# Attention gate bias on GpSimd: one operation on negated rows becomes two operations on rows as they are

## The chip, the core and the metric

The kernel runs on one core of a Trainium2 chip. The metric is device time in microseconds (us) of one execution. The core has four compute engines that run side by side and wait for each other through semaphores: PE (TensorE, matrix products; the profile lists its weight loads apart as PEld), DVE (VectorE), ACT (ScalarE) and POOL (GpSimd). SP issues the DMA transfers.

## What is computed

Two layers on 1024 tokens of width 1024. Layer 0 is a convolution module with a feed-forward net behind it, layer 1 an attention layer with another. The change lies in the attention, which has 16 heads of width 64 and a learned forget gate:

```python
log_f = log_sigmoid(f_logit + b_f)
c = cumsum(log_f, axis=1)                  # c[head, token]
s = q @ k.T                                # q is scaled by HEAD_DIM ** -0.5
bias = c[t] - c[s]                         # query t, key s
s = where(k_pos <= q_pos, s + bias, NEG_BIG)
o = softmax(s) @ v
```

## The kernel before, in words

`attention` works through 64 units: 8 head pairs p, in each four blocks u of 256 queries (from the longest row of keys to the shortest, in the last pair the other way round), and both heads e of the pair. A unit has two query tiles b of 128 queries; the tile i = 2u + b needs W = (i + 1) x 128 key columns, so W runs over 128, 256, ... 1024, each of them 16 times.

`gates` makes the cumulative gates once. `ctok` keeps them with tokens on partitions (128 x 8 x 16), and a transpose makes one row for each head, which goes to a buffer `cd` in DRAM (line 617 evacuates the transpose from PSUM, line 618 stores). For each head pair `gate_rows` loads each of the two rows from there, broadcast to 128 partitions, as `cb` (128 x 1024).

`scores` then does the softmax of a unit. For each of its two query tiles the work goes round the engines:

- POOL, line 709: z = row of gates + the query's gate (a column of 128 values), W columns. z is the buffer `pr`.
- POOL, line 710: the causal mask is added to the last 128 columns of z.
- PE, lines 718 and 719: two products of up to 512 columns into a PSUM tile `s` (three buffers).
- DVE, line 723: z = -(s + z) with the running minimum in `sm`; this frees `s`. Line 728 takes the smaller of two minima.
- ACT, line 729: exp, with the sum; DVE, line 730: its reciprocal.
- POOL, line 731: z times the reciprocal, times 1.0. Source and destination are the same buffer.

`values` follows a unit later: PE transposes the tiles (line 779, tile `t`), ACT and DVE split them into a high and a low part (`pt`, lines 111 and 112), POOL clears the part above the diagonal (line 781), and PE multiplies with V (line 749, tile `po`). In between, the units of pairs 0 to 6 are filled with the projections of the next pair (`psv`, `psq`, `psk`, line 137), which need no result of the softmax. Their weights pass through POOL too (line 125, times a gain). The last pair has no next one to project; it has the first part of the output product (`ps_wo`) beside and behind it.

Each engine runs its instructions in a fixed order. That order is not written in the code: a scheduler in the compiler lays it out from the units' priorities and from its own idea of how long each instruction takes, so an edit to one instruction can move others.

Of the kernel before, what the change touches and what calls it, by code (L numbers as in the profile page):

```python
# [14 lines left out]
ALU = mybir.AluOpType  # L15
# [7 lines left out]
HB = 512  # L23
# [36 lines left out]
class K:  # L60
# [521 lines left out]
    def gates(self, cd):  # L582

        nc = self.nc
        g = self.at.tile([P, T - P], F32, name="gate0", tag="pr0")
        gr = self.at.tile([P, T], F32, name="gate1", tag="pr1")
        u, e, lt, x = (g[:, i * P : (i + 1) * P] for i in range(4))
        z = self.zf.rearrange("p b n -> p (b n)")

        nc.vector.tensor_scalar(u, z, -1.0, None, ALU.mult)  # L590
        nc.vector.tensor_tensor(u, u, z, ALU.min)
        nc.scalar.activation(e, u, AF.Exp)
        nc.vector.tensor_scalar(u, e, 1.0, None, ALU.add)
        nc.scalar.activation(lt, u, AF.Ln)
        nc.vector.tensor_scalar(z, z, 0.0, None, ALU.min)
        nc.vector.tensor_tensor(z, z, lt, ALU.subtract)
        nc.vector.scalar_tensor_tensor(e, u, -1.0, e, ALU.add, ALU.subtract)
        nc.vector.reciprocal(lt, u)
        nc.vector.tensor_tensor(e, e, lt, ALU.mult)
        nc.vector.tensor_tensor(z, z, e, ALU.add)  # L600

        N = NHEAD
        nc.vector.tensor_copy(x[:, N : 2 * N], z[:, 0:N])
        for b in range(2, KT):
            c = b * N
            nc.vector.tensor_tensor(x[:, c : c + N], x[:, c - N : c], z[:, c - N : c], ALU.add)
        st = self.stp.tile([P, HB], F32, name="st_c", tag=self.stt)
        nc.tensor.matmul(st[:, 0:P], self.tri, z, start=True, stop=False)
        nc.tensor.matmul(st[:, N:P], self.ones, x[:, N:P], start=False, stop=True)
        ctok = self.cp.tile([P, KT, N], F32, name="ctok")  # L610
        nc.vector.tensor_copy(ctok.rearrange("p b n -> p (b n)"), st[:, 0:P])
        rows = gr[0:N, :]
        for h in range(NH):
            st = self.stp.tile([P, HB], F32, name=f"st_r{h}", tag=self.stt)
            for b in range(4):
                nc.tensor.transpose(st[0:N, b * P : (b + 1) * P], ctok[:, 4 * h + b, :], self.ident)
            nc.scalar.mul(rows[:, h * HB : (h + 1) * HB], st[0:N, :], -1.0)
        nc.sync.dma_start(cd, rows)
        return ctok

# [76 lines left out]
    def scores(self, cur, p, e, u):  # L697

        nc = self.nc
        n = 2 * p + e  # L700
        qk, ql = cur[p]
        cb = cur[p, "cb"][e]
        pr = [self.at.tile([P, T - (1 - b) * P], F32, name=f"pr{n}{u}{b}", tag=f"pr{b}") for b in range(2)]
        for b in range(2):
            i = 2 * u + b
            W = (i + 1) * P
            q = slice(i * P, W)
            z = pr[b][:, 0:W]
            nc.gpsimd.tensor_scalar(z, cb[:, 0:W], self.ctok[:, i, n : n + 1], None, ALU.add)  # L709
            nc.gpsimd.tensor_tensor(z[:, W - P : W], z[:, W - P : W], self.mask, ALU.add)  # L710
            sm = self.tp.tile([P, 8], F32, name=f"sm{n}{i}", tag="sm", bufs=6)
            m = 0
            for lo in range(0, W, HB):
                hi = min(lo + HB, W)
                cols = max(hi - lo, 256)
                ps = self.sp.tile([P, HB], F32, name=f"s{n}{i}{lo}", tag="s")
                kk = slice(lo, lo + cols)
                nc.tensor.matmul(ps[:, 0:cols], qk[:, e, q], qk[:, 2 + e, kk], start=True, stop=False)
                nc.tensor.matmul(
                    ps[:, 0:cols], ql[:, e, q], qk[:, 2 + e, kk], start=False, stop=True  # L720
                )
                zz = z[:, lo:hi]
                nc.vector.tensor_tensor_reduce(  # L723
                    zz, ps[:, 0 : hi - lo], zz, -1.0, 3.0e38, ALU.add, ALU.min, sm[:, m : m + 1]
                )
                m += 1
            if m == 2:
                nc.vector.tensor_tensor(sm[:, 0:1], sm[:, 0:1], sm[:, 1:2], ALU.min)  # L728
            nc.scalar.activation(z, z, AF.Exp, bias=sm[:, 0:1], scale=-1.0, accum_out=sm[:, 2:3])  # L729
            nc.vector.reciprocal(sm[:, 3:4], sm[:, 2:3])  # L730
            nc.gpsimd.tensor_scalar(z, z, sm[:, 3:4], 1.0, ALU.mult, ALU.mult)  # L731
        return pr
# [144 lines left out]
```

## Time and profile before

| what | value |
|---|---|
| three timed runs | 2718.55, 2723.5 and 2723.99 us, median 2723.5 us |
| the profiled execution, its own time | 2726.07 us |
| its span in the trace | 2724.3 us |
| mean granted clock of TensorE | 0.968 of full speed |
| busy share of the span: PE, DVE, ACT, POOL | 94%, 57%, 37%, 29% |
| units of attention, first to last line-709 instruction | 1243.8 to 1804.0 us |

The last row is the place of the change: 128 instructions of line 709 lie in some 560 us of the span, and POOL is all but idle after that. A busy share over the whole span says little there, so the rows below are cut to that stretch.

### The profile page before, as it was taken

To read this page: it belongs to the slowest core of one execution; us is meant where nothing else is said; L and a number is where in the kernel's file an instruction comes from. 1 tells how busy PE (TensorE), PEld (TensorE's weight loads), DVE (VectorE), ACT (ScalarE), POOL (GpSimd) and SP (SyncE) were. 2 spreads that over 40 slices of the span, in tenths; PEclk is the share of its full clock that TensorE was granted. 3 is DMA by queue.
4 is the path that set the end of the run, shared out by engine and by line. 5 is a ranking of instruction groups with operands and counts; after the bars stand their busy time and mean duration, and the time that the engine had idled before them with its cause. 6 is when DMAs were issued, how large, how long until landed. Compare 5 with 4: busy or idle time off the path is not lost.

```text
span 2724.3 us, 31354 instructions
## 1 busy us (share of the span) xinstructions
PE 2565.2 (94%) x12056; PEld 2133.0 (78%) x12056; DVE 1548.7 (57%) x2535; ACT 1005.9 (37%) x1608; POOL 780.1 (29%) x657
## 2 busy tenths in 40 slices
PE   7996999999999999989998898789999999999996
PEld 6875778888888888878777777568888888888885
DVE  7998999426644445555756666666422323223456
ACT  5245423223423334244545555544311302113232
POOL 3473534443000000025777777650000000000000
PEclk9997999999999999989999999789999999999998
DMA  3124222222222222222111111212111111111132
GB/s 127 54 78 155 70 90 89 105 96 88 99 101 93 101 94 100 74 98 71 47 40 47 40 53 55 103 54 79 48 54 47 47 49 52 47 47 51 54 112 108
DMA packets 63973, 205.25 MB, mean 75 GB/s; under 512 B 7360, under 2 KB 12096, under 8 KB 63312
## 3 DMA queue, kind: packets, MB, share of 16 engines
q1 hardware_dynamic: 62672, 199.06, 20.7%
q10 hardware_dynamic: 1152, 4.19, 0.4%
q8 instruction: 95, 1.56, 0.2%
q14 instruction: 54, 0.44, 0.0%
HBM read 182.71 MB, written 20.51 MB: 75 GB/s over the span
## 4 chain that ended last, share of the span: by engine, by line
PE 78%; DVE 10%; POOL 4%; issue 3%; ACT 2%; DMA 2%; POOLq 0%; DVEq 0%; SPq 0%; ACTq 0%
PE ps_fb L137 25%; PE ps_fa L137 24%; PE ps_gt L137 6%; PE ps_wo L137 3%; DVE ya L331 3%; PE pg L137 3%; PE pa L137 3%; PE psv L137 3%; PE psq L137 2%; PE psk L137 2%; POOL pr L709 2%; PE ps_pw L137 2%; PE t L779 1%; PE po L749 1%; DVE pr L723 1%
## 5 line engine op out<-in xcount | busy, mean ns | idle before, releaser
L204 POOL TENSOR_TENSOR r_g<-ms_g,mhalf 128x4 f32<-128x4 f32 x4 | 5.3, 1326 | 1041.6 <-DVE ms_g L202 1041.6
L331 DVE SCALAR_TENSOR_TENSOR ya<-u,wdw,ya 128x512 f32<-128x512 f32 x420 | 284.2, 746 | 0.0
L111 ACT CAST wh_fb<-raw_fb 128x1024 fp32r<-128x1024 f32 x96 | 101.0, 1054 | 412.2 <-PE ps_fb L137 295.3
L383 DVE SCALAR_TENSOR_TENSOR fa<-ps_fa,bs_f 128x512 f32<-128x512 f32 x128 | 88.0, 691 | 279.0 <-PE ps_fa L137 268.7
L111 ACT CAST wh_fa<-raw_fa 128x1024 fp32r<-128x1024 f32 x96 | 101.1, 1053 | 358.1 <-PE ps_fa L137 175.5
L709 POOL TENSOR_SCALAR pr<-cb,ctok 128x896 f32<-128x896 f32 (+7 forms) x128 | 223.5, 1755 | 33.8 <-PE t L779 29.2
L137 PE MATMUL ps_fa<-f10xl,wh_fa 128*128 128x512 f32 x512 | 199.4, 389 | 0.0
L137 PE MATMUL ps_fa<-f10xh,wl_fa 128*128 128x512 f32 x512 | 199.3, 389 | 0.0
L137 PE MATMUL ps_fa<-f10xh,wh_fa 128*128 128x512 f32 x512 | 199.0, 389 | 0.0
L389 DVE TENSOR_TENSOR hTb<-ps_fb,hTb 128x512 f32<-128x512 f32 x64 | 44.3, 692 | 233.3 <-PE ps_fb L137 233.3
L749 PE MATMUL po<-pt,V 128*128 128x256 f32 x640 | 127.7, 317 | 19.5 <-ACT pt L111 8.5
L385 ACT ACTIVATE fa<-fa 128x512 f32<-128x512 f32 x128 | 80.2, 629 | 153.3 <-DVE fa L383 153.3
L112 DVE TENSOR_TENSOR pt<-t,pt 128x512 fp32r<-128x512 f32 (+1 forms) x160 | 98.8, 633 | 62.6 <-ACT pt L111 62.0
L729 ACT ACTIVATE pr<-pr,sm 128x896 f32<-128x896 f32 (+7 forms) x128 | 99.3, 776 | 86.8 <-DVE sm L728 52.8
L389 DVE TENSOR_TENSOR hT<-ps_fb,hT 128x512 f32<-128x512 f32 x64 | 44.1, 690 | 147.7 <-PE ps_fb L137 147.7
L731 POOL TENSOR_SCALAR pr<-pr,sm 128x896 f32<-128x896 f32 (+7 forms) x128 | 101.6, 799 | 90.7 <-DVE sm L730 77.3
L779 PE MATMUL t<-ident,pr 128*128 128x128 f32 x576 | 103.6, 298 | 24.6 <-POOL pr L731 13.5
L749 PEld LDWEIGHTS po<-pt,V 128*128 128x128 f32 x640 | 98.6, 205 | 34.8 <-ACT pt L111 14.5
L723 DVE CUSTOM_DVE_ANT_0 pr<-s,pr 128x512 f32<-128x512 f32 (+3 forms) x192 | 104.0, 552 | 36.4 <-POOL pr L710 14.8
L111 ACT CAST pt<-t 128x512 fp32r<-128x512 f32 (+1 forms) x160 | 84.1, 543 | 87.1 <-PE t L779 83.9
L137 PEld LDWEIGHTS ps_fa<-f10xl,wh_fa 128*128 128x128 f32 x512 | 96.1, 188 | 20.0
L137 PEld LDWEIGHTS ps_fa<-f10xh,wh_fa 128*128 128x128 f32 x512 | 96.1, 188 | 20.0
(356 smaller groups left out, 7430.8 us busy)
## 6 DMA issues: line engine op xcount, KB each, us to landing
raw_fa<-in_wf SPq DMA_DIRECT2D x96, 512.0 KB, 3.2
raw_fb<-in_wf SPq DMA_DIRECT2D x96, 512.0 KB, 3.2
raw_gt<-in_wgate SPq DMA_DIRECT2D x24, 512.0 KB, 3.2
proj<-pj SPq DMA_DIRECT2D x32, 256.0 KB, 2.2
raw_pw<-in_wpw SPq DMA_DIRECT2D x16, 512.0 KB, 3.3
lpj<-proj SPq DMA_DIRECT2D x32, 256.0 KB, 3.2
cb<-cd SPq DMA_DIRECT2D x16, 512.0 KB, 3.9
raw_wo<-in_wo SPq DMA_DIRECT2D x16, 320.0 KB, 2.8
```

What stands on the lines that cost most here:

```text
L111: copy(h, src)
L112: sub.tensor_tensor(l, src, h.bitcast(F32), ALU.subtract)
L137: self.nc.tensor.matmul(ps, p[:, k, :], q[:, k, :], start=(start and k == k0 and n == 0), stop=(stop and k == kt - 1 and n == 2),)
L331: nc.vector.scalar_tensor_tensor(d, s(j), w(j), o, ALU.mult, ALU.add)
L383: nc.vector.scalar_tensor_tensor(t, ps, 0.0, s[h][1], ALU.max, ALU.mult)
L389: nc.vector.tensor_tensor(hT[h][:, j, :], ps, hT[h][:, j, :], ALU.add)
L709: nc.gpsimd.tensor_scalar(z, cb[:, 0:W], self.ctok[:, i, n : n + 1], None, ALU.add)
L723: nc.vector.tensor_tensor_reduce(zz, ps[:, 0 : hi - lo], zz, -1.0, 3.0e38, ALU.add, ALU.min, sm[:, m : m + 1])
L729: nc.scalar.activation(z, z, AF.Exp, bias=sm[:, 0:1], scale=-1.0, accum_out=sm[:, 2:3])
L731: nc.gpsimd.tensor_scalar(z, z, sm[:, 3:4], 1.0, ALU.mult, ALU.mult)
L749: nc.tensor.matmul(po, V[:, j, n % 4, :], pt[:, q, c : c + 256], start=(j == 0 and q == 0), stop=(jp == u and jj == 1 and q == 1),)
L779: nc.tensor.transpose(ps[:, c : c + P], pr[b][:, j * P : (j + 1) * P], self.ident)
```

## The change

Line 617 stores the gate rows as they are, no longer times minus one. Line 709 makes up for it: it multiplies the row by minus one and adds the query's gate, in one instruction. Both forms give c[t] - c[s].

```diff
@@ gates
-            nc.scalar.mul(rows[:, h * HB : (h + 1) * HB], st[0:N, :], -1.0)
+            nc.scalar.copy(rows[:, h * HB : (h + 1) * HB], st[0:N, :])
@@ scores
-            nc.gpsimd.tensor_scalar(z, cb[:, 0:W], self.ctok[:, i, n : n + 1], None, ALU.add)
+            nc.gpsimd.tensor_scalar(z, cb[:, 0:W], -1.0, self.ctok[:, i, n : n + 1], ALU.mult, ALU.add)
             nc.gpsimd.tensor_tensor(z[:, W - P : W], z[:, W - P : W], self.mask, ALU.add)
```

The number of instructions of the two lines stays: 2 of line 617 on ACT, 128 of line 709 on POOL. No buffer, transfer or wait is added. The scheduler's order does change on all engines from the first unit on. Two places show how.

On POOL, at the start of attention (head pair 0; `pr030` is head 0, u = 3, b = 0, `raw_q1` and `raw_k1` are weights of the next pair; the number behind the last underscore only tells buffers apart). A minus is the order before, a plus the order of the change:

```order
 L709 TENSOR_SCALAR pr030_8715<-cb0_8711,ctok_8553 128x896
 L709 TENSOR_SCALAR pr031_8716<-cb0_8711,ctok_8553 128x1024
+L710 TENSOR_TENSOR pr030_8715<-pr030_8715,mask_8154 128x128
 L709 TENSOR_SCALAR pr130_8816<-cb1_8713,ctok_8553 128x896
 L709 TENSOR_SCALAR pr131_8817<-cb1_8713,ctok_8553 128x1024
+L710 TENSOR_TENSOR pr031_8716<-pr031_8716,mask_8154 128x128
 L125 TENSOR_TENSOR raw_q1_9273<-raw_q1_9273,vec_66 128x1024
-L710 TENSOR_TENSOR pr030_8715<-pr030_8715,mask_8154 128x128
-L710 TENSOR_TENSOR pr031_8716<-pr031_8716,mask_8154 128x128
```

The two masks of the first unit move ahead of the weights of the next pair, and so do the scores that wait for them.

On POOL, at the end of attention (head pair 7, u = 3, its longest rows):

```order
 L709 TENSOR_SCALAR pr1430_14222<-cb14_13909,ctok_8553 128x896
 L709 TENSOR_SCALAR pr1431_14223<-cb14_13909,ctok_8553 128x1024
+L731 TENSOR_SCALAR pr1521_14148<-pr1521_14148,sm155_14166 128x768
+L710 TENSOR_TENSOR pr1430_14222<-pr1430_14222,mask_8154 128x128
+L710 TENSOR_TENSOR pr1431_14223<-pr1431_14223,mask_8154 128x128
 L781 MEMSET pt1522_14283 128x2x128
 L709 TENSOR_SCALAR pr1530_14295<-cb15_13911,ctok_8553 128x896
 L709 TENSOR_SCALAR pr1531_14296<-cb15_13911,ctok_8553 128x1024
-L710 TENSOR_TENSOR pr1430_14222<-pr1430_14222,mask_8154 128x128
-L710 TENSOR_TENSOR pr1431_14223<-pr1431_14223,mask_8154 128x128
```

Here the masks of head 14 no longer stand behind the two line-709 instructions of head 15.

## Rows read from the trace of the kernel before

**Rows 1.** The page's busy line; then busy us by engine, clock, DMA in three stretches:

```profile
span 2724.3 us, 31354 instructions
...
PE 2565.2 (94%) x12056; PEld 2133.0 (78%) x12056; DVE 1548.7 (57%) x2535; ACT 1005.9 (37%) x1608; POOL 780.1 (29%) x657
...
1225.00:1825.00 600.00, 525.10 (x2945) 440.16 (x2944) 382.91 (x967) 314.38 (x641) 438.70 (x467) 0.93 0.16 56
1275.00:1675.00 400.00, 360.35 (x2099) 306.29 (x2098) 257.88 (x645) 211.87 (x428) 302.19 (x317) 0.97 0.12 42
1675.00:1825.00 150.00, 115.63 (x531) 89.40 (x530) 97.33 (x266) 79.53 (x177) 112.37 (x135) 0.81 0.24 87
```

**Rows 2.** Chain of work that ended last, share by line, 1225-1825 us and 1675-1825 us:

```profile
by line: PE psq L137 10.5%; PE psk L137 10.3%; POOL pr L709 8.5%; issue 8.1%; PE psv L137 7.9%; PE t L779 5.8%; PE po L749 5.6%; DVE pr L723 3.2%; PE s L718 3.1%; POOL pr L731 3.1%; PE s L719 2.7%; PE ps_wo L137 2.6%; DVE pt L112 2.3%; ACT 
by line: POOL pr L709 10.9%; PE ps_wo L137 10.3%; issue 7.9%; DMA raw_o<-od 6.8%; PE psk L137 5.4%; POOL pr L731 5.2%; PE po L749 5.2%; DMA cb<-cd 5.0%; PE t L779 4.4%; DVE pr L723 4.3%; DMA od<-o 4.0%; DVE xol L112 3.9%; ACT pr L729 3.7%; 
```

**Rows 3.** Lines 709 and 731, whole and by shape: count, busy us, mean ns, idle before:

```profile
L709 POOL TENSOR_SCALAR pr<-cb,ctok 128x896 f32<-128x896 f32 (+7 forms) x128 | 223.5, 1755 | 33.8 <-PE t L779 29.2
...
L731 POOL TENSOR_SCALAR pr<-pr,sm 128x896 f32<-128x896 f32 (+7 forms) x128 | 101.6, 799 | 90.7 <-DVE sm L730 77.3
...
L709 POOL TENSOR_SCALAR pr<-cb,ctok 128x1024 f32<-128x1024 f32 x16 | 45.6, 2850 | 0.0
L709 POOL TENSOR_SCALAR pr<-cb,ctok 128x512 f32<-128x512 f32 x16 | 25.1, 1566 | 0.6 <-PE t L779 0.6
L709 POOL TENSOR_SCALAR pr<-cb,ctok 128x128 f32<-128x128 f32 x16 | 9.7, 608 | 8.3 <-PE t L779 6.6 <-DMA cb<-cd 1.7
L731 POOL TENSOR_SCALAR pr<-pr,sm 128x1024 f32<-128x1024 f32 x16 | 18.9, 1181 | 25.8 <-DVE sm L730 19.9 <-DVE sm L728 5.6
L731 POOL TENSOR_SCALAR pr<-pr,sm 128x512 f32<-128x512 f32 x16 | 11.4, 712 | 7.1 <-DVE sm L730 7.1
L731 POOL TENSOR_SCALAR pr<-pr,sm 128x128 f32<-128x128 f32 x16 | 6.1, 379 | 2.8 <-DVE sm L730 2.7
```

**Rows 4.** Other two-input POOL instructions by shape, adding (323, 710) and multiplying (304, 300):

```profile
L323 POOL TENSOR_TENSOR y<-y,cm 128x512 f32<-128x512 f32 x30 | 42.8, 1426 | 5.1 <-ACT cm L321 3.5
L304 POOL TENSOR_TENSOR ta<-ta,bs_n 128x512 f32<-128x512 f32 x16 | 24.2, 1514 | 20.6 <-ACT ta L303 20.6
L300 POOL TENSOR_TENSOR sg<-sg,bs_n 128x512 f32<-128x512 f32 x16 | 21.2, 1322 | 12.1 <-ACT sg L299 8.8 <-ACT bs_n L210 3.3
L710 POOL TENSOR_TENSOR pr<-pr,mask 128x128 f32<-128x128 f32 x128 | 64.1, 512 | 0.0
```

**Rows 5.** Timeline of POOL late in attention: start, duration, line:

```profile
1781.35 2.21 POOL L709 TENSOR_SCALAR pr<-cb,ctok 128x768 f32<-128x768 f32 x1
1783.54 0.70 POOL L731 TENSOR_SCALAR pr<-pr,sm 128x512 f32<-128x512 f32 x1
1784.20 0.88 POOL L710 TENSOR_TENSOR pr<-pr,mask 128x128 f32<-128x128 f32 x2
1785.06 1.89 POOL L709 TENSOR_SCALAR pr<-cb,ctok 128x640 f32<-128x640 f32 x1
1786.89 0.31 POOL L781 MEMSET pt<- 128x256 f32 x1
1787.18 2.21 POOL L709 TENSOR_SCALAR pr<-cb,ctok 128x768 f32<-128x768 f32 x1
```

**Rows 6.** Waits in attention: engine and line, released by, total us, times, longest:

```profile
PE s L718 <- DVE sm L723: 21.3, 25, 3.5
PE t L779 <- POOL pr L731: 13.5, 16, 2.5
PE t L779 <- DVE pt L112: 8.7, 21, 1.3
PE po L749 <- ACT pt L111: 8.5, 13, 1.6
...
DVE pr L723 <- POOL pr L710: 14.8, 22, 2.1
DVE pr L723 <- POOL pr L709: 9.0, 11, 1.5
```

**Rows 7.** ACT: the evacuation at line 617, and a plain copy from PSUM:

```profile
L617 ACT ACTIVATE gate<-st_r x2: 589/589/589, 1234.4 to 1237.1; 16x512 f32<-16x512 f32 x2
...
L299 ACT COPY sg<-pg 128x512 f32<-128x512 f32 x16 | 9.3, 580 | 22.6 <-PE pg L137 20.5 <-DVE acc_n L196 1.8 <-DVE u L305 0.3
```

## Prediction

> **What bounds the kernel now.** I read first the busy line of the page, then the busy time cut to the stretch in which line 709 runs [rows 1]. Over the whole span POOL is busy 29% and looks harmless. Between 1225 and 1825 us it is busy 438.7 of 600 us, second only to PE with 525.1. PE therefore stands idle 600 - 525.1 = 74.9 us there. That is the most that any change to the softmax's side work can return as idle time. The idle time is uneven: 400 - 360.4 = 39.6 us between 1275 and 1675 us, where the projections of the next pair fill PE, and 150 - 115.6 = 34.4 us between 1675 and 1825 us, where that filling gives out. There the granted clock also falls to 0.81, from 0.97.
>
> Next I read the chain of waits, to see whether POOL's busy time sits on the path that sets the end [rows 2]. It does: line 709 has 8.5% of the chain in the 600 us, or 51.0 us, and 10.9% of the 150 us at the end, or 16.4 us, where it is the largest entry of all. Last I read who waits for POOL [rows 6]. PE waits for line 731 before its transposes (13.5 us), and for line 723 to free a score tile (21.3 us). Line 723 itself is held by lines 710 and 709 (14.8 and 9.0 us). So line 709 hurts mostly through what is queued behind it on POOL, not by direct waits.
>
> **What the change removes, step by step.** *The bias instruction.* Line 709 takes 223.5 us of POOL in 128 instructions; line 731 has the same eight shapes, 16 of each, and takes 101.6 us [rows 3]. Both are a POOL tensor_scalar on f32 in SBUF with a column operand. From 128 to 1024 columns line 709 goes from 608 to 2850 ns, 2.50 ns a column; line 731 goes from 379 to 1181 ns, 0.90 ns a column. So on this engine the form with two operations is already seen to be the cheaper one, by almost three times a column. The question is which difference between the two lines makes it so. They differ in the number of operations (one against two), in the kind (add against multiply), in the buffer (from `cb` to `pr` against in place), and in the place of the column operand. The new form agrees with line 731 in the number of operations and in its first operation; it differs in the other three.
>
> The kind alone is a poor explanation: on two-input instructions of 512 columns an add takes 1426 ns and two multiplies 1322 and 1514 ns [rows 4], so adding isn't dearer as such. Contention for the memory is a poor one too: late in attention, line 709 with 768 columns takes 2.21 us both times, and the next instruction starts right behind it, so the duration is real, and a line-731 instruction of 512 columns in between takes 0.70 us under the same neighbours [rows 5]. In place or not, and where the column stands, no row separates.
>
> So the bounds for the new form are: below, line 731's 101.6 us in all; above, a generic loop that pays for each operation, up to twice line 709's price a column. Twice means 2.50 ns x 576 columns on average x 128 = 184 us more. I take the lower bound, since line 731 is the nearest row in every respect that changes: 223.5 - 101.6 = 121.9 us less POOL, 54.5% of line 709.
>
> The Trainium skill has a rule that speaks against this. GPSIMD Engine Reference, section Performance versus the Vector engine, says that a loop with up to two operations an element runs at the memory port's rate, 1.03 cycles an element, and gets slower only from three on. By it a second operation can't make anything faster, and line 709 should already cost what line 731 does; a change of the operation count would then return nothing. The trace agrees for line 731 and disagrees for line 709, which takes nearly three times as long; the measurement decides that the one-operation form isn't at that rate here, but not why.
>
> *The path.* Of the 51.0 us of line 709 on the chain, 54.5% go: 27.8 us. Two things are left out on either side. What is late next takes some of it back: the transposes also wait for line 112 (8.7 us) and the products with V for line 111 (8.5 us) [rows 6], and a shorter POOL step uncovers them. Against that, PE waits less and may keep its clock in the last 150 us, where 0.81 is granted. I set these two equal. For the range, half of the 27.8 us (14) is lost to the next waits at worst, and at best two thirds of PE's idle time (50 us) come back.
>
> *The gate rows.* Line 617 becomes a copy, twice in the program. It took 589 ns as a multiply; a plain copy from PSUM with the same 512 columns takes 580 ns [rows 7]. I count nothing; even 1 us each would be hidden, as PE still has projections to run there.
>
> *The order.* The scheduler moves instructions on all engines. On POOL the masks move ahead of the second head's line 709 and ahead of the weights of the next pair. Each shift puts at most two or three POOL instructions before another, some 2 to 5 us by rows 3 and 4, and it shortens the way to line 723 as often as it delays weights, so I count nothing and keep +-5 us for the range.
>
> **The sum.** 2726.1 - 27.8 = 2698.3 us for the profiled execution. That one lies 2.6 us above the median of the three timed runs, so the forecast for a median is 2723.5 - 27.8 = 2696 us, 1.0% faster. About 0.2%, 5 us, is what a measurement of this kernel can tell from no change.
>
> **The rivals.**
>
> *The second operation costs extra (slower).* Line 709 may be slow because its add with a column runs in a generic loop; the new form then stays in that loop and pays for another operation. At line 731's 0.90 ns a column this adds 0.90 x 576 x 128 = 66 us of POOL, 23% of which reach the chain as now (51.0 / 223.5): +15 us, 2739 us. At double price POOL would need 438.7 + 184 = 623 us in the 600 us: it becomes the bound, and by its share of the chain +42 us, 2766 us. It decides as soon as the new form costs more than 2.50 ns a column by some 0.3 (5 us at the chain's share). For it: lines 709 and 731 differ in three more things than the count. Against it: no row shows a POOL tensor_scalar with two operations slower than one.
>
> *The duration doesn't change.* Slowness comes from reading one buffer and writing another, or from the column added to; this is what the rule above would leave as the cause. Then only the order moves: 2723 us, 5 either way.
>
> *Faster on POOL, nothing at the end.* The POOL step shortens, but PE is then held by lines 111 and 112 and by the single `po` tile. For it: PE is already 88% busy in the stretch. Against it: in the last 150 us line 709 tops the chain and PE idles 34.4 us, so that 16.4 x 0.545 = 9 us should return there alone. It gives 2718 to 2724 us.
>
> **How the numbers follow.** The forecast with its gain above 5 us: 0.70, with its own range 2674 to 2710 us (50 and 14 us of gain). Extra cost: 0.12. Unchanged duration: 0.10, of which 0.06 within 0.2%, and 0.02 to each side from the order. Faster POOL without effect: 0.08, of which 0.01 ends slower. So faster 0.70 + 0.02 = 0.72, same 0.06 + 0.07 = 0.13, slower 0.12 + 0.02 + 0.01 = 0.15. The range is 2674 to 2730 us: below it some 0.05, above it the extra cost, 0.12 and a little.
>
> **What would show it.** In the profile of the changed kernel: line 709 at some 800 ns mean and 100 us in all, with 1.2 us for 1024 columns; POOL some 317 us busy in the attention stretch; line 709's share of the chain there halved; PE idle some 50 us in place of 74.9, most of the gain spread over 1275 to 1675 us and a third in the last 150; line 731's duration unchanged. The forecast is wrong if line 709 stays above 1.7 us on average (first or second rival), or if it falls and PE's waits for lines 111, 112 and 723 grow by as much (the third).

## The result, and the profile after

The changed kernel takes 2640.4 us (2639.8 to 2641.8, four runs), where the kernel before takes 2722.3 us (four runs): a ratio of 0.970, with a 95% interval of 0.9685 to 0.9719. It is 82 us faster. The forecast had the direction and the instruction right, but only a third of the gain, and the time lies below its range.

The page and the rows by shape of the kernel after answer to [rows 1] and [rows 3]:

```profile
span 2640.1 us, 31431 instructions
...
PE 2524.8 (96%) x12056; PEld 2113.2 (80%) x12056; DVE 1545.3 (59%) x2535; ACT 1002.3 (38%) x1608; POOL 660.7 (25%) x657
...
L731 POOL TENSOR_SCALAR pr<-pr,sm 128x896 f32<-128x896 f32 (+7 forms) x128 | 98.1, 768 | 101.0 <-DVE sm L730 94.9
...
L709 POOL TENSOR_SCALAR pr<-cb,ctok 128x896 f32<-128x896 f32 (+7 forms) x128 | 105.6, 830 | 36.6 <-PE t L779 31.0
...
L709 POOL TENSOR_SCALAR pr<-cb,ctok 128x1024 f32<-128x1024 f32 x16 | 20.3, 1271 | 0.0
L709 POOL TENSOR_SCALAR pr<-cb,ctok 128x512 f32<-128x512 f32 x16 | 13.8, 863 | 0.0
L709 POOL TENSOR_SCALAR pr<-cb,ctok 128x128 f32<-128x128 f32 x16 | 8.7, 544 | 4.1 <-PE t L779 2.2 <-DMA cb<-cd 1.9
```

Line 709 falls from 223.5 to 105.6 us, 117.9 us less, where 121.9 was forecast; line 731 stays. So the step on the instruction holds. The surprise is elsewhere. Next, busy us by engine, granted clock and DMA of the kernel after in its attention stretch, in the part that projections fill and in the part where they give out:

```profile
1225.00:1740.00 515.00, 485.25 (x2938) 420.88 (x2937) 379.94 (x964) 310.79 (x640) 318.28 (x467) 0.98 0.19 65
1275.00:1600.00 325.00, 316.92 (x1971) 279.32 (x1971) 239.96 (x594) 196.38 (x402) 206.85 (x293) 1.00 0.16 53
1600.00:1740.00 140.00, 118.75 (x627) 95.74 (x626) 106.60 (x294) 86.88 (x193) 85.53 (x147) 0.91 0.26 93
```

The stretch that took 600 us before, up to the end of line 709 and a little more, takes 515 us now, with all but the same number of PE products in it (2938 against 2945). PE's idle time falls from 74.9 to 515 - 485.3 = 29.8 us. That is 45 us; the other 40 us come from PE's busy time itself, 525.1 to 485.3 us, for the same work. The clock goes with it: the mean granted clock of the stretch rises from 0.93 to 0.98 of 2.4 GHz, which is a mean over that level and the one of 1.2 GHz. By the clock records of the two traces, PE was busy for 69 us of its 525 at the lower level before, and for 21 of its 485 now. In the kernel before, a product of line 749 takes 462 ns at the lower level and 300 ns at the upper one on average, and the other lines that ran at both take 1.5 to 1.7 times as long at the lower. An estimate from these numbers is that the rise of the clock accounts for 16 to 20 of the 40 us; where the rest comes from is not shown. The prediction took its best case from the idle time alone; a product that runs at the lower level counts as busy, for longer.

Share of the chain by line from 1240 to 1730 us, and PE's waits from 1225 to 1800 us, of the kernel after:

```profile
by line: PE psk L137 15.8%; PE psq L137 14.6%; PE psv L137 11.4%; PE po L749 10.5%; PE t L779 9.0%; PE s L718 5.2%; PE s L719 4.7%; DVE pt L112 3.9%; issue 3.2%; DVE pr L723 3.2%; DVE qk L692 2.4%; ACT pt L111 2.3%; POOL pr L709 2.0%; POOL 
```

```profile
PE s L718 <- DVE sm L723: 8.5, 14, 1.2
PE po L749 <- ACT pt L111: 7.5, 11, 1.7
PE t L779 <- DVE pt L112: 4.8, 10, 1.1
PE t L779 <- POOL pr L731: 4.5, 7, 1.9
```

Line 709 has 2.0% of the chain, against 8.5% before [rows 2]. PE waits 8.5 us for line 723 in place of 21.3, and 4.5 us for line 731 in place of 13.5 [rows 6]. The waits for lines 111 and 112, which were expected to grow, shrink from 17.2 to 12.3 us.

### The profile page after: what moved, and what is told of

Read it like the earlier page. It is cut to its first block, busy times and chain, and to the rows that moved or that the text cites. A ratio compares the mean times of both kernels' runs of the same rounds, so it can differ in the third digit from the quotient of the medians.

```text
span 2640.1 us, 31431 instructions
## 1 busy us (share of the span) xinstructions
PE 2524.8 (96%) x12056; PEld 2113.2 (80%) x12056; DVE 1545.3 (59%) x2535; ACT 1002.3 (38%) x1608; POOL 660.7 (25%) x657
## 4 chain that ended last, share of the span: by engine, by line
PE 84%; DVE 10%; POOL 2%; ACT 2%; issue 2%; DMA 1%; DVEq 0%; POOLq 0%; SPq 0%; ACTq 0%
PE ps_fb L137 26%; PE ps_fa L137 25%; PE ps_gt L137 6%; PE ps_wo L137 3%; PE psq L137 3%; DVE ya L331 3%; PE psv L137 3%; PE pg L137 3%; PE psk L137 3%; PE pa L137 3%; PE po L749 2%; PE t L779 2%; PE ps_pw L137 2%; PE s L718 1%; PE s L719 1%
## 5 line engine op out<-in xcount | busy, mean ns | idle before, releaser
L749 PE MATMUL po<-pt,V 128*128 128x256 f32 x640 | 121.3, 305 | 9.4 <-ACT pt L111 7.5
L723 DVE CUSTOM_DVE_ANT_0 pr<-s,pr 128x512 f32<-128x512 f32 (+2 forms) x192 | 103.4, 550 | 22.7 <-POOL pr L710 12.4
L709 POOL TENSOR_SCALAR pr<-cb,ctok 128x896 f32<-128x896 f32 (+7 forms) x128 | 105.6, 830 | 36.6 <-PE t L779 31.0
L137 PEld LDWEIGHTS ps_fa<-f10xh,wl_fa 128*128 128x128 f32 x512 | 96.1, 188 | 19.9
L749 PEld LDWEIGHTS po<-pt,V 128*128 128x128 f32 x640 | 92.4, 195 | 18.2 <-ACT pt L111 11.9
```

The lines of the kernel that those rows point to most:

```text
L137: self.nc.tensor.matmul(ps, p[:, k, :], q[:, k, :], start=(start and k == k0 and n == 0), stop=(stop and k == kt - 1 and n == 2),)
L709: nc.gpsimd.tensor_scalar(z, cb[:, 0:W], -1.0, self.ctok[:, i, n : n + 1], ALU.mult, ALU.add)
L723: nc.vector.tensor_tensor_reduce(zz, ps[:, 0 : hi - lo], zz, -1.0, 3.0e38, ALU.add, ALU.min, sm[:, m : m + 1])
L749: nc.tensor.matmul(po, V[:, j, n % 4, :], pt[:, q, c : c + 256], start=(j == 0 and q == 0), stop=(jp == u and jj == 1 and q == 1),)
```

## The experiments

The change does two things at once: it makes an instruction shorter, and it makes the scheduler lay out another order on every engine. The first four kernels take these apart. Three of them use a trick: the program is laid out with one form of line 709, and then each of the 128 instructions is exchanged for another form, in its place, with the same waits:

```diff
+def reform(nc):
+    for f in nc.m.functions:
+        for blk in f.blocks:
+            for k, i in enumerate(blk.instructions):
+                if "TensorScalarPtr" in type(i).__name__ and i.op0 == ALU.add and i.op1 == ALU.bypass:
+                    if i.engine == mybir.EngineType.Pool:
+                        x, c = i.ins
+                        one = mybir.ImmediateValue(dtype=F32, value=1.0)
+                        blk.instructions[k] = copy.replace(i, ins=[x, one, c], op0=ALU.mult, op1=ALU.add)
...
         build(tc, aps)
+    reform(nc)
```

**The shorter instruction in the old order** (the edit above on the kernel before; its gate rows stay negated, so that the factor is 1.0):

> The program is laid out with the one-operation form, so every engine has the order of the kernel before; then each of the 128 line-709 instructions is exchanged in place for the form with two operations (times 1.0, plus gate; the rows stay negated). Only the duration changes. Theory A (the shorter instruction is what returns the time): line 709 at some 105 us in all as in the changed kernel, and 2640 to 2660 us. Theory B (the new order returns more than half): 2695 us, the 27.8 us that the chain's share gave, or slower. Theory C (order and duration must fit each other): between, 2660 to 2690 us.

It took 2705.8 us (ratio 0.9935, 0.9920 to 0.9951): 18 us faster, though line 709 is down to 100.8 us. Theories A and C miss; B's "or slower" allows it. The duration alone returns less than the 27.8 us of the chain's share. Line 709 in this kernel:

```profile
L709 POOL TENSOR_SCALAR pr<-cb,ctok 128x896 f32<-128x896 f32 (+7 forms) x128 | 100.8, 792 | 53.1 <-PE t L779 48.5 <-DMA cb<-cd 3.8
```

**The old instruction in the new order.** The line in `scores` is `tensor_scalar(z, cb[:, 0:W], 1.0, self.ctok[:, i, n : n + 1], ALU.mult, ALU.add)` on negated rows, and the exchange goes the other way:

```diff
+                if "TensorScalarPtr" in type(i).__name__ and i.op0 == ALU.mult and i.op1 == ALU.add:
+                    if i.engine == mybir.EngineType.Pool:
+                        x, one, c = i.ins
+                        blk.instructions[k] = copy.replace(i, ins=[x, c], op0=ALU.add, op1=ALU.bypass)
```

> The reverse: the program is laid out with the two-operation form, so every engine has the order of the changed kernel; then each line-709 instruction is exchanged for the one-operation add on negated rows. Theory A: line 709 at some 223 us again, and 2715 to 2730 us, as before. Theory B: 2665 to 2695 us, most of the gain stays. Theory C: slower than before, above 2730 us.

2712.3 us (0.9959, 0.9944 to 0.9974): 12 us faster than before. That falls to none of the three: it lies just below theory A's range and far from those of B and C. The order alone doesn't hold the gain either. So duration alone gives 18 us, order alone 12, and both together 82: some 50 us belong to neither alone. Where they come from shows in the chain. Share by line from 1240 to 1800 us of this kernel (slow form, new order), from its first line-709 instruction to its last:

```profile
by line: POOL pr L709 33.1%; issue 9.7%; POOL pr L731 6.1%; DVE pr L723 5.0%; POOL pr L710 4.8%; PE t L779 4.5%; PE psv L137 4.2%; ACT pr L729 2.5%; PE psk L137 2.4%; PE s L718 2.4%; PE s L719 1.8%; DMA raw_q<-in_wq 1.8%; PE po L749 1.7%; D
```

and from 1240 to 1790 us of the kernel above (short form, old order):

```profile
by line: PE psk L137 10.5%; PE psv L137 9.7%; PE po L749 9.1%; PE psq L137 8.0%; PE t L779 7.3%; issue 6.5%; DVE pr L723 5.1%; DVE pt L112 4.8%; ACT pt L111 3.3%; PE s L718 3.1%; ACT pr L729 3.1%; PE s L719 2.7%; DMA raw_o<-od 2.5%; DVE o L
```

In the new order with the slow form, line 709 has 33.1% of 560 us, 185 us, against 8.5% of 600 us, 51 us, in the kernel before [rows 2]. POOL's timeline at the start of the second pair shows the run of it (start, duration, line):

```profile
1329.64 2.97 POOL L709 TENSOR_SCALAR pr<-cb,ctok 128x896 f32<-128x896 f32 x1
1332.69 0.46 POOL L710 TENSOR_TENSOR pr<-pr,mask 128x128 f32<-128x128 f32 x1
1333.13 2.85 POOL L709 TENSOR_SCALAR pr<-cb,ctok 128x1024 f32<-128x1024 f32 x1
1336.06 0.46 POOL L710 TENSOR_TENSOR pr<-pr,mask 128x128 f32<-128x128 f32 x1
1336.50 3.19 POOL L731 TENSOR_SCALAR pr<-pr,sm 128x896 f32<-128x896 f32 x2
```

The two line-709 instructions of one unit take 5.8 of the first 10 us, and the rest of POOL's work stands behind them. Here line 709 has the largest share of the chain. The short form takes 52% off it, so the chain foretells 97 us; 2712 - 2640 = 72 us is what it returned. In the old order the chain foretold 28 us, and 18 came. So in both orders the chain's share foretold more than came back, by a third to a half. And it is a price for one order; the change brought another, in which the same instruction held more than three times as much. In the old order with the short form, line 709 has left the chain's first entries; products, lines 111, 112 and 723 and the "issue" time lead it.

**Two short instructions in place of one** (the new line 709 written twice):

> The changed kernel with line 709 issued twice in a row into the same buffer (the second has the same inputs and writes the same values), so POOL carries 2 x 105 = 211 us for it, close to the 223.5 us of before, in the fast form; the scheduler lays the program out anew. Theory A (POOL's time alone counts): most of the gain is gone, 2700 to 2730 us. Rival D (the slow form does harm beyond its own duration, to DVE's reads for instance): 2640 to 2670 us.

2697.2 us (0.9906, 0.9888 to 0.9924), just below theory A's range, with POOL busy 427.9 us between 1225 and 1825 us, all but the 438.7 of before. Most of the gain is gone, so there is no need for a special harm of the slow form; line 723 on DVE takes 550 ns after and 552 before. That it is 27 us below before with nearly the same load on POOL may be the order again, as this one was laid out anew; no run separates that.

**Half of the short instructions in the old order** (the first edit on every second instruction):

> As the first kernel, in the order of the kernel before, but only every second line-709 instruction is exchanged for the two-operation form (64 of 128). POOL gets back half of what it gets back there. If each us of POOL returns the same, half of that kernel's gain; if POOL's queue holds the others only when it is nearly full, more than half of the gain comes with this first half; if the gain needs both tiles of a unit to be early, less than a third.

2713.2 us (0.9958, 0.9942 to 0.9973): 11 of the 18 us come with the first half. Every second instruction is here the first tile of each unit, the shorter of the two (896 columns take 1.05 us, 1024 columns still 2.96), so POOL got back 52 of the 123 us, and in proportion that would be 8 us of time. The five runs lie between 2706.7 and 2715.0 us, so that more than this came back isn't clear of the noise. The third reading, less than a third of the gain, is refuted.

**Which forms are short.** A third order came from the form plus gate, plus 0.0. It was run with the short form put in its place:

> A third order with the same fast instruction: the program is laid out with line 709 as plus gate, plus zero, and each is then exchanged in place for times 1.0, plus gate. In this order 1237 of the 1600 attention products of PE stand in groups of 20 or more without a projection between them, against 1067 in the order of before and 769 in that of the changed kernel. If what is left after the shorter instruction is set by how finely projections are laid between the attention products, this lies at or above the 2706 us of the order of before: 2705 to 2725 us. If the order of before is merely an unlucky one, or the groups don't matter, 2640 to 2690 us.

and as it is, `tensor_scalar(z, cb[:, 0:W], self.ctok[:, i, n : n + 1], 0.0, ALU.add, ALU.add)`:

> Line 709 as two operations that both add: plus gate, plus 0.0, rows negated as before. If two operations are what makes the instruction short: line 709 at some 105 us in all and the time of order_add_zero within 5 us. If the first operation must be a multiplication: 223 us or more, and 2720 to 2760 us.

2765.4 us (1.0156, 1.0140 to 1.0172) and 2789.2 us (1.0245, 1.0225 to 1.0264). The first has the same short instruction as the changed kernel (102.3 us in all) and is 125 us slower, far above both ranges given: an order, by itself, made that. Line 709 in it, and PE's longest waits from 1225 to 1825 us; the 39.1 us for line 723 stand against 8.5 us in the changed kernel:

```profile
L709 POOL TENSOR_SCALAR pr<-cb,ctok 128x1024 f32<-128x1024 f32 x16 | 19.7, 1232 | 2.7 <-PE t L779 2.5
...
PE s L718 <- DVE sm L723: 39.1, 31, 5.7
PE t L779 <- DVE pt L112: 16.6, 29, 2.2
```

The second, 29 us above the top of its range, shows that two operations are not enough. The rows of 1024 and 128 columns in it:

```profile
L709 POOL TENSOR_SCALAR pr<-cb,ctok 128x1024 f32<-128x1024 f32 x16 | 59.3, 3704 | 0.0
L709 POOL TENSOR_SCALAR pr<-cb,ctok 128x128 f32<-128x128 f32 x16 | 11.4, 716 | 5.9 <-PE t L779 5.5 <-DMA cb<-cd 0.4
```

1024 columns take 3.7 us, against 2.85 us for one addition [rows 3] and 1.27 us for the new form. Two more forms:

> Line 709 as plus gate, times 1.0, rows negated as before; the order on every engine is that of the changed kernel. If two operations of any kind are enough: some 105 us for line 709 and 2640 us. If the order mult, add or the column in second place matters: 223 us for line 709 and 2712 us, as with the one-operation form in this order.

This was `tensor_scalar(z, cb[:, 0:W], self.ctok[:, i, n : n + 1], 1.0, ALU.add, ALU.mult)`: 2642.7 us in a single run, and short:

```profile
L709 POOL TENSOR_SCALAR pr<-cb,ctok 128x1024 f32<-128x1024 f32 x16 | 20.4, 1274 | 0.0
```

Line 617 stays a multiplication in this kernel, and the order is that of the changed kernel; the 2 us of difference are no more than a single run leaves open, so no effect of the edit to the gate rows is seen, as forecast. The last form was line 731 as `tensor_scalar(z, z, sm[:, 3:4], None, ALU.mult)` in the changed kernel:

> The changed kernel with line 731 cut to one operation (times the reciprocal, without times 1.0); it stays in place and a multiplication. If the number of operations alone makes the instruction slow, line 731 goes from 98 us to some 220 us and the time to 2680 to 2720 us. If working in place or multiplying is what makes it fast, line 731 stays at 98 us and the time at 2640 us.

2687.7 us in a single run, and line 731 is slow though it works in place and multiplies:

```profile
L731 POOL TENSOR_SCALAR pr<-pr,sm 128x1024 f32<-128x1024 f32 x16 | 45.5, 2844 | 9.3 <-DVE sm L730 8.3 <-DVE sm L728 0.9
L731 POOL TENSOR_SCALAR pr<-pr,sm 128x128 f32<-128x128 f32 x16 | 10.0, 628 | 1.9 <-DVE sm L730 1.9
```

So of six forms, the three with two operations of which one is a multiplication are short (some 0.8 to 0.9 ns a column); one addition, one multiplication, and two additions are not (2.50, 2.47 and 3.33 ns). Why a multiplication makes the difference, no run shows.

**What sets an order's time.** By now three orders with equally short instructions took 2640, 2706 and 2765 us. In them 769, 1067 and 1237 of PE's 1600 attention products stand in groups of 20 or more with no projection between (attention products are those into `s`, `t` and `po`). Four kernels tested that count by moving only where `attention` draws pieces of the projections, or the order of the query blocks:

```diff
@@ fill_two
                 next(fills[0], None)
+                if i % 8 < 4:
+                    next(fills[0], None)
@@ fill_first
+                next(fills[0], None)
                 late.append((self.scores(cur, p, e, u), cur, p, e, u))
                 if len(late) > 1:
                     self.values(*late.pop(0), o, od)
-                next(fills[0], None)
@@ fill_coarse
-                next(fills[0], None)
+                if i % 2:
+                    next(fills[0], None)
+                    next(fills[0], None)
@@ units_mixed
-            units = [(p, e, u) for p in range(NP) for u in ((0, 1, 2, 3) if p == NP - 1 else (3, 2, 1, 0)) for e in range(2)]
+            units = [(p, e, u) for p in range(NP) for u in ((0, 1, 2, 3) if p == NP - 1 else (3, 0, 2, 1)) for e in range(2)]
```

> The changed kernel, with the projections of the next pair drawn two pieces per unit in the first four units of a pair, so that they are used up early; every instruction and its duration stay. In the order that comes of it, 1003 of PE's 1600 attention products stand in groups of 20 or more without a projection between them (769 in the changed kernel, 1067 and 1237 in the two slower orders at the same durations, which took 2706 and 2765 us). If these groups set what is lost: between 769 at 2640 and 1067 at 2706 us, that is 2692 us, from 2675 to 2710. If they are only a companion of something else: 2635 to 2660 us.

> The changed kernel, with a piece of the projections drawn ahead of the unit's scores instead of behind its values; durations as they are. 665 of the 1600 attention products stand in groups of 20 or more. If the groups set the loss: 2617 us by the same line, faster than the changed kernel, 2610 to 2638 us. If not: 2640 us or slower.

> The changed kernel, with two pieces drawn in every second unit instead of one in each. 842 of the 1600 in groups of 20 or more. By the line 2656 us, from 2645 to 2670; if the groups don't matter 2640 us.

> The changed kernel, with the query blocks of a pair in the order 3, 0, 2, 1 instead of 3, 2, 1, 0, so that long rows of keys alternate with short ones on POOL. 764 of the 1600 in groups of 20 or more, as many as in the changed kernel. If the groups alone set the loss: 2640 us within 8; if POOL's share of a unit matters as well, some other way off by more than 15 us.

2656.3 us (0.9747, 0.9731 to 0.9764), 2641.2 us (0.9695, 0.9678 to 0.9713), and 2650.4 and 2640.8 us in single runs. The last two agree with the count, the first two don't: it foretold 2692 us where 2656 was measured, and 2617 where 2641 was. So the count doesn't set the loss. All four orders, laid out with the short form, lie within 16 us of the changed kernel; the time rises with the count there, but 1003 go with 2656 us and the 1067 of the old order with 2706. The two orders that were laid out with a slow form and then run with the short one lie 65 and 125 us above the changed kernel.

That suggests a fit between an order and the durations for which it was laid out. The last three kernels measured what a microsecond of POOL is worth in either order.

> The order of the changed kernel, with every second line-709 instruction (64 of 128) exchanged in place for the one-operation form. If POOL sets the pace of this order (line 709 had 33.8% of the chain of 1240 to 1660 us with the slow form), the time is about half way between 2640 and 2712 us, in proportion to POOL's time: 2665 to 2688 us. If the order needs all instructions short (any late one holds the rest), close to 2712 us; if it has slack, close to 2640 us.

> The order of the changed kernel, each line-709 instruction exchanged in place for plus gate, plus 0.0, which took 287.9 us in all where one operation takes 223.5. If POOL sets the pace, the slope of 72 us of time for 118 us of POOL goes on: 64 us more are 39 us more, 2751 us, from 2740 to 2775. If the chain's share of the order of before held here (23% of line 709), 2727 us.

> The order of the kernel before, each line-709 instruction exchanged in place for plus gate, plus 0.0 (287.9 us in all). If this order is held by more than POOL, its slope stays small: 18 us of time for 118 us of POOL give 10 us more, 2734 us, from 2728 to 2745. If POOL becomes the bound, as the rival on a costlier second operation had it, 2739 us and above, up to 2760.

| form of line 709 | old order: line 709 in all, time | new order | third order |
|---|---|---|---|
| short | 101 us, 2705.8 us | 106 us, 2640.4 us | 102 us, 2765.4 us |
| short in the first tile of each unit | 172 us, 2713.2 us | 171 us, 2667.3 us | not run |
| one addition | 224 us, 2722 to 2726 us (the kernel before) | 222 us, 2712.3 us | not run |
| two additions | 286 us, 2752.6 us | 285 us, 2776.8 us | 288 us, 2789.2 us |

Half short in the new order lies in the range given for a pace set by POOL, but at its lower end: in proportion to POOL's time it would be 2681 us. The two others lie above what the slopes foretold (2751 and 2734 us). They have ratios of 0.9789 (0.9774 to 0.9803), 1.0192 (1.0177 to 1.0207) and 1.0098 (1.0082 to 1.0115), for half short and two additions in the new order, and two additions in the old. In the new order the time rises by 0.4, 0.9 and 1.0 us for each us of POOL; in the old one by 0.1, 0.2 and 0.5, the first two not clearly apart. Each order has a time of its own with the short form and a slope above it. The old order has the higher time and the gentler slope; the two cross where line 709 takes some 240 us.

The table speaks against the fit, as far as real durations go. The old order was laid out for one addition, yet with one addition the new order is 12 us faster. The third was laid out for two additions, yet with two additions it is the slowest of the three. Only with the short form is the order that was laid out for it the best.

With two additions the new order is the slower one, by 24 us, and its chain holds more of line 709 than of anything else (1240 to 1860 us):

```profile
by line: POOL pr L709 37.8%; issue 9.2%; PE t L779 5.3%; POOL pr L731 5.2%; DVE pr L723 4.5%; PE psk L137 4.0%; PE psv L137 4.0%; POOL pr L710 3.9%; PE s L718 3.1%; PE s L719 2.3%; PE po L749 2.1%; PE psq L137 1.9%; ACT pr L729 1.7%; DMA ra
```

## Why the prediction was wrong

**The bias instruction.** Right: 117.9 us less on POOL against 121.9, with the bound that was chosen. The number of operations was a property that counts, but not alone: of the forms tried, only those in which one of the two multiplies are short. One reading of the code was wrong: lines 709 and 731 both had the column operand in the first place, so its place was never a difference between them, and the runs with it in either place are equally short (1274 and 1271 ns for 1024 columns). The costlier rival's price, 0.90 ns a column more, was real for another form: two additions cost 0.83 ns a column more than one.

**The rule of the Trainium skill** that was weighed (GPSIMD Engine Reference, Performance versus the Vector engine: up to two operations run at the port's rate) doesn't hold for these instructions: one operation took 2.5 ns a column and two took 0.8 to 0.9 or 3.3, by their kind.

**The path.** 27.8 us from the chain's share. In the order for which that chain was read the short form returned 18 us: the central value was a third of itself too large for that order, though 18 lies between the 14 and 50 us that the range allowed. That part was only mis-sized.

**The order.** This is the step that failed. "I count nothing and keep +-5 us for the range": the order alone is worth 12 us, and it turns the short instruction's 18 us into 2712 - 2640 = 72 us. With the same short instruction the new order is 65 us faster than the old one. The prediction looked at two places where POOL instructions change places and priced each shift by the instructions passed. The runs show that the layout of all engines together can be worth tens of us either way; they don't show which part of it did it. Nothing in the prediction could tell a layout like the new one from one like the third, which is 125 us slower with the same instruction.

**The best case and the clock.** The best case was put at two thirds of PE's idle 74.9 us, 50 us. The idle time gave 45 us, but busy time gave another 40, by the estimate above about half of it through the higher granted clock, a term that was set to nothing against the next waits. PE's idle time was no upper bound here.

**The rivals.** Extra cost, unchanged duration and no effect are all refuted for the form that was built.

**Still open:** which property of an order sets its time with the short form, and its slope. Groups of attention products foretell little of it. That a layout fits the durations assumed in it agrees, by the real durations, with the short form alone and not with one or two additions; how long the scheduler takes each form to be wasn't looked at. An order is here the whole layout, the sequence on every engine with its waits; the order of one engine alone wasn't exchanged.

## What to carry to other kernels

When an edit makes a scheduler lay out another order, that order is a term of the sum of its own, of either sign, and the chain of the kernel before prices the edit in the old order only. Separate the two: keep the order and exchange the instruction, or keep the instruction and exchange the order; here the halves gave 18 and 12 us and the whole 82. A layout's time couldn't be foretold here, so try several: with the same instruction they took from 2640 to 2765 us here. And on GpSimd, for f32 in SBUF as measured here, give a tensor_scalar with a column operand a second operation, one of the two a multiplication, even if it multiplies by one.

## What the runs showed of the hardware

A GpSimd tensor_scalar on f32 with 1024 columns takes 1.1 to 1.3 us on average with two operations of which one multiplies, 2.8 to 3.0 us with one operation, addition or multiplication, and 3.7 us with two additions. The same instruction isn't quite constant: 512 columns of the short form read 863 ns in the changed kernel and 693 ns in the third order, beside other neighbours; the cause wasn't tried.
